# The w_out product as seven block products in a one-core encoder step

## The chip, the cores and the metric

The kernel runs on one core of one Trainium2 chip. The metric is the device time of one execution in microseconds (us). One core has five engines that work at once: TensorE (PE, matrix products into PSUM banks), VectorE (DVE), ScalarE (ACT), GpSimd (POOL) and SyncE (SP), which here only issues transfers (DMAs). Each engine, and each queue of DMAs, takes its own instructions in a fixed order.

## The reference

One layer of a streaming encoder over 1024 prompt tokens and 64 sample tokens: norm, one input projection, two attention branches, and then the part that matters here:

```python
def merge_and_ffn(x, oa, ob, ga, gb, w_o_a, w_o_b, w_out, norm_ffn, w_up, w_down):
    B, T, _ = x.shape
    m = ga * (oa.reshape(B, T, W_A) @ w_o_a) + gb * (ob.reshape(B, T, W_B) @ w_o_b)
    x = x + m @ w_out
    h = jnp.square(jax.nn.relu(rmsnorm(x, norm_ffn) @ w_up))
    return x + h @ w_down
```

`m` and `x` have 1024 + 64 rows of 1024, `w_out` is 1024 x 1024, and everything is float32.

## The kernel before

A float32 product is made of three passes: each operand is split into a rounded part `hi` and the rest `lo` (`split`, L145: ACT copies to `hi`, then POOL or DVE subtracts to get `lo`), and `three` (L152) issues hi·hi, hi·lo and lo·hi for each block of 128 in the inner dimension k. The 64 sample rows are held as hi and lo side by side in one block of 128 columns ("few"), so they need two passes.

The stages around the change, in order of time:

- **Merge** (L960 to L989). For each block m of 128 model columns and each of three chunks of tokens, two products into the PSUM tile `acc` (six banks), a DVE multiplication by each gate (L978), a POOL sum of the two branches (L981), and a split of the sum into `mT` (L988 on ACT, L989 on DVE).
- **Out product** (L1063 to L1093). `together` takes 512 columns of w_out at a time, and for each of eight blocks k runs all row tiles of a group: rows 0 to 3 and the sample rows, or rows 4 to 7 (a row tile is 128 tokens). `in_turn` takes the last two strips of 256 columns for rows 4 to 7, one row tile after the other. Weights come through the pool `ring`: `raw` has 3 buffers, `hi` and `lo` 5 each; POOL makes `lo`. `take` adds a finished PSUM tile to the residual tile `x1[i]` on DVE (L1057).
- **Norm and transposes** (`ffn_columns`, L1023). A row tile whose 1024 columns are complete is stored, squared and summed on ACT (L172), scaled on DVE (L174), transposed by PE in two groups of four (L1034, PSUM tile `pt`, two banks), and ACT copies each group twice: to `turned` (two buffers), which a DMA on ACT's queue stores, and, for rows 0 to 3 and the first 32 sample rows, to the operands B11 and B21 of the next product (names with `xB`), whose `lo` DVE makes (L1042).
- **Up product** (L1109 on). It is already a product by seven blocks. Its first products, in the PSUM tiles `pf`, `pa` and `pe`, need B11 complete: rows 0 to 3 and the sample rows. Rows 4 to 7 are only needed much later.

The order of instructions on each engine is set when the kernel is built, by a scheduler that may move an instruction ahead of others that it takes to be waiting; the pools decide which buffer a tile gets, and thereby what it waits for.

## Time and profile before

| what | us |
| --- | --- |
| median of 3 runs (1688.88 to 1691.14) | 1690.06 |
| the profiled execution | 1689.98 |
| its span, first to last instruction | 1687.8 |
| PE busy in the span | 1671.8 |
| first matmul of the out product, from the span's start | 910.54 |
| first matmul of the up product | 1011.64 |

All times of the trace count from the span's start. What an execution takes beyond the span is 1689.98 - 1687.8 = 2.2 us. A row of the timeline gives the start, the duration, the engine, the line and the operation, out<-in; a matmul's duration overlaps the next one's, so what a matmul costs is read from one start to the next. A row of the stages gives the busy time of each engine between two times, then the granted TensorE clock (1.00 is full speed), the share of the DMA engines and the GB/s. "DMA to landing" is the time from the issue of a transfer to its arrival.

### The profile page before, as it was taken

To read this page: it belongs to the slowest core of one execution; us is meant where nothing else is said; L and a number is where in the kernel's file an instruction comes from. 1 tells how busy PE (TensorE), PEld (TensorE's weight loads), DVE (VectorE), ACT (ScalarE), POOL (GpSimd) and SP (SyncE) were. 2 spreads that over 40 slices of the span, in tenths; PEclk is the share of its full clock that TensorE was granted. 3 is DMA by queue.
4 is the path that set the end of the run, shared out by engine and by line. 5 is a ranking of instruction groups with operands and counts; after the bars stand their busy time and mean duration, and the time that the engine had idled before them with its cause. 6 is when DMAs were issued, how large, how long until landed. Compare 5 with 4: busy or idle time off the path is not lost.

```text
span 1687.8 us, 29807 instructions
## 1 busy us (share of the span) xinstructions
PE 1671.8 (99%) x10181; PEld 1525.1 (90%) x10181; DVE 1165.4 (69%) x2732; ACT 936.1 (55%) x1874; POOL 388.6 (23%) x524
## 2 busy tenths in 40 slices
PE   9899999999999999999999999999999999999999
PEld 8887888888989999999999899999999988888887
DVE  6854899878868788873553346756687649656794
ACT  6866578795167777774443446544454346443431
POOL 4344223504533434332344430000000000000000
PEclk9999999999999999999999999999999999999999
DMA  7234365673498876645545459555565598765652
GB/s 248 62 123 136 99 182 161 181 252 100 114 217 205 201 178 158 161 113 177 166 136 168 171 168 303 170 178 178 188 223 188 191 294 300 238 202 172 204 187 87
DMA packets 278119, 303.06 MB, mean 180 GB/s; under 512 B 40208, under 2 KB 196368, under 8 KB 277968
## 3 DMA queue, kind: packets, MB, share of 16 engines
q1 hardware_dynamic: 248704, 265.44, 53.6%
q10 hardware_dynamic: 29264, 35.73, 6.0%
q8 instruction: 80, 1.31, 0.3%
q14 instruction: 71, 0.58, 0.1%
HBM read 207.98 MB, written 93.08 MB: 178 GB/s over the span
## 4 chain that ended last, share of the span: by engine, by line
PE 79%; DMA 3%; DVE 3%; issue 1%; POOL 1%; ACT 1%; SPq 0%; DVEq 0%; ACTq 0%; POOLq 0%
PE acc L156 7%; PE acc L158 7%; PE acc L157 7%; PE x L158 6%; PE x L157 6%; PE x L156 6%; PE pt L817 3%; PE wide L158 2%; PE wide L157 2%; PE wide L156 2%; PE pg L156 2%; PE pg L158 2%; PE pg L157 2%; PE pe L156 2%; PE pe L158 2%; PE po L833 2%
## 5 line engine op out<-in xcount | busy, mean ns | idle before, releaser
L124 ACT ACTIVATE hi<-hw 128x1024 fp32r<-128x1024 f32 (+1 forms) x108 | 100.2, 933 | 158.3 <-PE x L158 51.0
L157 PE MATMUL x<-lo,hi 128*128 128x512 f32 (+1 forms) x440 | 169.5, 385 | 0.0
L158 PE MATMUL x<-hi,lo 128*128 128x512 f32 (+1 forms) x440 | 169.1, 385 | 0.0
L156 PE MATMUL x<-hi 128*128 128x512 f32 (+1 forms) x440 | 165.1, 385 | 0.0
L148 DVE TENSOR_TENSOR lo<-hw,hi 128x1024 fp32r<-128x1024 f32 (+1 forms) x108 | 114.0, 1061 | 48.6 <-ACT hi L124 46.5
L150 POOL TENSOR_TENSOR lo<-raw,hi 128x512 fp32r<-128x512 f32 x74 | 96.9, 1315 | 127.0 <-ACT hi L124 112.4
L124 ACT ACTIVATE hi<-raw 128x512 fp32r<-128x512 f32 x104 | 65.1, 627 | 91.1 <-PE acc L157 21.6
L622 ACT ACTIVATE nth<-work,cand 128x768 bf16<-128x768 f32 (+2 forms) x93 | 96.6, 1038 | 15.9 <-DVE cand L640 9.6
L829 DVE TENSOR_TENSOR pl<-pt,ph 128x512 fp32r<-128x512 f32 (+2 forms) x152 | 91.6, 616 | 14.5 <-ACT ph L124 14.0
L157 PEld LDWEIGHTS x<-lo,hi 128*128 128x128 f32 x440 | 82.7, 188 | 16.6
L156 PEld LDWEIGHTS x<-hi 128*128 128x128 f32 x440 | 82.6, 188 | 16.7 <-ACT hi L124 0.2
L158 PEld LDWEIGHTS x<-hi,lo 128*128 128x128 f32 x440 | 82.6, 188 | 16.5
L156 PE MATMUL acc<-xnT,hi 128*128 128x384 f32 (+1 forms) x288 | 96.2, 334 | 0.2 <-DVE gate L688 0.2
L124 ACT ACTIVATE ph<-pt 128x512 fp32r<-128x512 f32 (+3 forms) x168 | 80.9, 514 | 26.1 <-PE pt L817 16.4
L158 PE MATMUL acc<-xnT,lo 128*128 128x384 f32 (+1 forms) x288 | 94.3, 327 | 0.0
L157 PE MATMUL wide<-wlo,xnT 128*128 128x512 f32 x240 | 94.2, 394 | 0.0
L157 PE MATMUL acc<-xnT,hi 128*128 128x384 f32 (+1 forms) x288 | 94.2, 327 | 0.0
L158 PE MATMUL wide<-whi,xnT 128*128 128x512 f32 x240 | 93.8, 391 | 0.0
L156 PE MATMUL wide<-whi,xnT 128*128 128x512 f32 x240 | 92.2, 394 | 0.9 <-DVE work_s L383 0.9
L804 POOL TENSOR_SCALAR mw<-mw,sm 128x640 f32<-128x640 f32 (+1 forms) x64 | 56.6, 885 | 122.7 <-DVE sm L803 118.3
L833 PE MATMUL po<-pl,vhl 128*128 128x256 f32 (+1 forms) x304 | 79.0, 291 | 0.7 <-DVE pl L829 0.7
L832 PE MATMUL po<-ph,vhl 128*128 128x256 f32 (+1 forms) x304 | 78.6, 275 | 0.3 <-ACT ph L124 0.2
(700 smaller groups left out, 5612.0 us busy)
## 6 DMA issues: line engine op xcount, KB each, us to landing
hw<-h SPq DMA_DIRECT2D x108, 256.0 KB, 3.1
hw<-in_w_down_dram SPq DMA_DIRECT2D x108, 256.0 KB, 3.5
wraw<-in_w_in_dram SPq DMA_DIRECT2D x56, 256.0 KB, 2.8
h<-h ACTq DMA_DIRECT2D x32, 272.0 KB, 2.1
raw<-in_w_out_dram SPq DMA_DIRECT2D x32, 256.0 KB, 2.7
raw<-in_w_up_dram SPq DMA_DIRECT2D x32, 256.0 KB, 3.1
out_dram<-t SPq DMA_DIRECT2D x24, 256.0 KB, 2.5
raw<-in_w_in_dram SPq DMA_DIRECT2D x24, 256.0 KB, 3.6
```

Source lines behind the costliest of these rows:

```text
L124: return nc.scalar.activation(out, in_, AF.Copy)
L148: last["lo"] = nc.vector.tensor_sub(lo, raw, hi)
L150: nc.gpsimd.tensor_sub(lo, raw, hi)
L156: nc.tensor.matmul(out, sh, mh, start=(opens and i == 0), stop=False, skip_group_check=resumes)
L157: nc.tensor.matmul(out, sh, ml, start=False, stop=False, skip_group_check=resumes)
L158: last = nc.tensor.matmul(out, sl, mh, start=False, stop=(closes and i == n - 1), skip_group_check=resumes)
L622: nc.scalar.activation(sign[:, :w.shape[1]], w, AF.Sign, bias=against, scale=-1.0, accum_out=col(cnt, j))
L804: nc.gpsimd.tensor_scalar(m[:rows, :n], m[:rows, :n], sm[:rows, 6:7], 1.0, op0=ALU.mult, op1=ALU.mult)
L817: nc.tensor.transpose(ps[:krows, oo:oo + qrows], m[:qrows, kc:kc + krows], ident[:qrows, :qrows])
L829: nc.vector.tensor_sub(pl[:kr, a:b], ps[:kr, a:b], ph[:kr, a:b])
L832: nc.tensor.matmul(dst, vhl[:krows, vt, :], ph[:krows, oo:oo + width], start=(idx == 0), stop=False)
L833: nc.tensor.matmul(dst, vhl[:krows, vt, :], pl[:krows, oo:oo + width], start=False, stop=(idx == n - 1))
```

## The change

The 1024 prompt rows of `m`, and w_out, are cut into two by two blocks of 512. Instead of eight block products, seven are made: P1 and P2 from the blocks themselves, the other five from sums of left blocks and sums of right blocks. Each is four row tiles by 512 columns by four blocks k. They run in the order P1, P2, P6, P5, P3, P7, P4; P1, P6, P5, P3 follow each other in the same four PSUM banks without being cleared, so that a bank holds P1, then P1 + P6, and so on, and DVE adds it to the rows that need it at each stage (`into`). P2 goes through the two `pt` banks. P7 and P4 are chained in the same way. The sample rows keep eight small matmuls a block product, in P1, P2, P3 and P7.

The sums of left blocks are made in the merge stage by DVE (`left_sums`, after each pair of blocks m), from `m_of`, which keeps `m` unsplit; they are split one block product ahead of their use (`left_side`). The sums of right blocks are made from the freshly loaded weights (`right_side`); `t1_of` and `t2_of` keep two of them from one product to the next. The residual rows are loaded by `load_rows`, rows 0 to 3 and the sample rows with P1, rows 4 to 7 with P2. All of rows 4 to 7 now get their last addition only from P4, and all four are normed behind it. Some pools change sides.

On DVE, at the end of the merge stage (`gta` and `gtb` are the gates, `m_...` the kept blocks of `m`, `x_0` the first residual row tile), before:

```order
L978 TENSOR_TENSOR gta<-acc,gta 128x320
L989 TENSOR_TENSOR mT_11321<-gtb,mT_11321 128x256
L989 TENSOR_TENSOR mT_11322<-gtb,mT_11322 128x64
L1057 TENSOR_TENSOR x_0_12353<-acc,x_0_12353 128x512
L1057 TENSOR_TENSOR x_1_12354<-acc,x_1_12354 128x512
```

and after (`tc` is a tile of `t1_of`, `raw` a block of w_out):

```order
L1002 TENSOR_TENSOR gta<-acc,gta 128x320
L961 TENSOR_TENSOR s_3_11337<-m_11329,m_11333 128x512
L965 TENSOR_TENSOR m_11329<-m_11329,m_11333 128x64
L955 TENSOR_TENSOR few_m<-m_11333,few_m 128x64
L962 TENSOR_TENSOR m_11329<-m_11329 128x512
L955 TENSOR_TENSOR few_m<-m_11329,few_m 128x64
L963 TENSOR_TENSOR m_11329<-s_3_11337,m_11329 128x512
L148 TENSOR_TENSOR lo<-m_11326,hi 128x512
L1105 TENSOR_TENSOR tc<-tc,raw 128x512
```

The last reader of P1's first block of weights (L1105) now stands behind the left sums of the last pair.

On SP's queue, from the w_out blocks of the first product on (`x_0` to `x_8` are the residual row tiles, `x_8` the sample rows), before:

```order
L1050 DMA raw<-in_w_out_dram 128x512 x4
L1009 DMA x_0_12353<-in_x_prompt_dram 128x1024
L1009 DMA x_1_12354<-in_x_prompt_dram 128x1024
L1009 DMA x_2_12355<-in_x_prompt_dram 128x1024
L1009 DMA x_3_12356<-in_x_prompt_dram 128x1024
L1011 DMA x_8_12357<-in_x_sample_dram 64x1024
L1009 DMA x_4_12349<-in_x_prompt_dram 128x1024
L1009 DMA x_5_12350<-in_x_prompt_dram 128x1024
L1009 DMA x_6_12351<-in_x_prompt_dram 128x1024
L1009 DMA x_7_12352<-in_x_prompt_dram 128x1024
L1050 DMA raw<-in_w_out_dram 128x512 x14
```

and after:

```order
L1040 DMA tc<-in_w_out_dram 128x512 x4
L1034 DMA x_0_12344<-in_x_prompt_dram 128x1024
L1034 DMA x_1_12345<-in_x_prompt_dram 128x1024
L1034 DMA x_2_12346<-in_x_prompt_dram 128x1024
L1040 DMA raw<-in_w_out_dram 128x512
L1034 DMA x_3_12347<-in_x_prompt_dram 128x1024
L1036 DMA x_8_12348<-in_x_sample_dram 64x1024
L1034 DMA x_4_12340<-in_x_prompt_dram 128x1024
L1034 DMA x_5_12341<-in_x_prompt_dram 128x1024
L1034 DMA x_6_12342<-in_x_prompt_dram 128x1024
L1034 DMA x_7_12343<-in_x_prompt_dram 128x1024
L1040 DMA raw<-in_w_out_dram 128x512 x16
```

Before, all eight blocks k of the first pass stand ahead of the residual rows. After, P1's fourth block stands between `x_2` and `x_3`, and all of P2's blocks behind `x_7`.

On PE, at the end of the out product (`pt` are transposes, `pf` the first up product), before:

```order
L158 MATMUL acc<-hi,mT_11321 128x256
L1034 MATMUL pt<-ident,xg 128x128 x8
L156 MATMUL pf<-xB_of_x,hi 128x272
L157 MATMUL pf<-xB_of_x,hi 128x272
L158 MATMUL pf<-xB_of_x,lo 128x272
```

and after:

```order
L158 MATMUL acc<-hi,lo 128x512
L1067 MATMUL pt<-ident,xg 128x128 x16
L1067 MATMUL pt<-ident,xg 128x64 x8
L156 MATMUL pf<-xB_of_x,hi 128x272
L157 MATMUL pf<-xB_of_x,hi 128x272
L158 MATMUL pf<-xB_of_x,lo 128x272
```

Before, the eight transposes there are of row tile 4, which the up product does not need yet. After, row tiles 2 and 3 and the sample rows are transposed between the last block product and the up product, which needs them. On ACT, in the same place after (`junk` is the square of a row tile, `sd` its root, `hi` a weight of the up product):

```order
L172 ACTIVATE junk,ss<-x_5_12341 128x1024
L124 ACTIVATE hi<-raw 128x512 x2
L132 ACTIVATE sd<-ss,eps 128x1
L124 ACTIVATE turned<-pt 128x512
L124 ACTIVATE xB_of_x<-pt 128x4x128
L172 ACTIVATE junk,ss<-x_6_12342 128x1024
L124 ACTIVATE turned<-pt 128x512
L124 ACTIVATE xB_of_x<-pt 128x4x128
L132 ACTIVATE sd<-ss,eps 128x1
L172 ACTIVATE junk,ss<-x_7_12343 128x1024
L1077 DMA xT_74<-turned 128x8x128
L124 ACTIVATE turned<-pt 128x512
```

The copies of row tile 2 (the `turned` and `xB` rows here) stand among the squares of row tiles 5, 6 and 7; row tile 3 and the sample rows follow.

The core of the diff:

```diff
+    pairs_of_m = tuple(m for k in range(4) for m in (k, k + 4))
...
+    def left_sums(k):
+        a, b = m_of[k], m_of[k + 4]
+        a1, a2, b1, b2 = a[:, :512], a[:, 512:1024], b[:, :512], b[:, 512:1024]
+        nc.vector.tensor_add(s1_of[k], a2, b2)
+        nc.vector.tensor_sub(a2, a1, a2)
+        nc.vector.tensor_sub(a1, s1_of[k], a1)
+        nc.vector.tensor_sub(b1, b1, a1)
+        nc.vector.tensor_add(a[:, 1024:], a[:, 1024:], b[:, 1024:])
+        few_block(2, k, a[:, 1024:])
...
+            nc.gpsimd.tensor_add(m_of[m][:, c0:c0 + n], prods[1][:, :n], prods[0][:, :n])
+            if ci == 1:
+                hi, lo = (row_blocks["A11" if m < 4 else "A12"][:, m % 4, z] for z in range(2))
+                copied = copy(hi, m_of[m][:, :512])
+                nc.vector.tensor_sub(lo, m_of[m][:, :512], hi)
+            elif ci == 2:
+                copied = few_block(m // 4, m % 4, m_of[m][:, 1024:])
+                if m >= 4:
+                    left_sums(m - 4)
...
+    def right_side(nm, k):
+        hi = ring.tile([P, 512], F32R, tag="hi", name="hi", bufs=RING)
+        lo = ring.tile([P, 512], F32R, tag="lo", name="lo", bufs=RING)
+        if nm == "P1":
+            t = out_block(k, 0, 0)
+            out_block(k, 0, 1, t1_of[k])
...
+        split(t, hi, lo)
+        if nm == "P1":
+            nc.vector.tensor_sub(t1_of[k], t1_of[k], t)
+        return hi, lo
...
+    ops = sides("P1")
+    load_rows(first_rows)
+    sums, few_sum = [acc() for _ in range(4)], acc()
+    by_halves(sums, ops, True, (few_sum, 0, True))
+    for t in range(4):
+        into(t, 0, sums[t])
+    ops = sides("P2")
+    load_rows(second_rows)
+    for t in range(4):
+        ps = ptile()
+        tile_product(ps, t, ops, range(4), True)
+        into(t, 0, ps)
...
+    sums = [acc() for _ in range(4)]
+    by_halves(sums, sides("P7"), True, (few_sum, 3, False))
+    for t in range(2):
+        ffn_columns(t)
+    ops = sides("P4")
+    for t in range(2, 4):
+        ffn_columns(t)
+    into(NT, 1, few_sum)
+    ffn_columns(NT)
+    for t in range(4):
+        into(4 + t, 1, sums[t])
+    by_halves(sums, ops, False)
+    for t in range(4):
+        into(4 + t, 0, sums[t])
...
-    together(first_rows, 0)
-    together(first_rows, 512)
-    together(second_rows, 0)
-    in_turn(second_rows, 512)
-    in_turn(second_rows, 768)
...
     with tc.issue_after(begin(0, "pf").ins):
+        ffn_columns(4)
         ffn_columns(5)
```

## The prediction

> **What bounds the kernel now.** I read the page first, then the stages around the out product, then the timeline of single engines there.

> ```profile
> span 1687.8 us, 29807 instructions
> PE 1671.8 (99%) x10181; PEld 1525.1 (90%) x10181; DVE 1165.4 (69%) x2732; ACT 936.1 (55%) x1874; POOL 388.6 (23%) x524
> ```

> PE is the bound by share, and the stages say that this holds here too. The rows are the merge, the out product and the start of the up product; after the stretch stand its length, then PE's busy time, PE's weight loads, DVE, ACT, POOL, the granted clock, the share of the DMA engines and GB/s.

> ```profile
> 820.00:912.90 92.90, 92.90 (x564) 92.48 (x563) 49.99 (x90) 39.75 (x99) 45.59 (x42) 1.00 0.42 128
> 912.90:1011.00 98.10, 98.10 (x545) 85.41 (x544) 34.12 (x77) 41.45 (x81) 38.15 (x30) 1.00 0.59 194
> 1011.00:1030.00 19.00, 18.92 (x156) 18.54 (x154) 10.19 (x21) 11.78 (x23) 0.67 (x1) 1.00 0.85 245
> ```

> PE has no gap in the out product and 0.08 us after it, at full clock. So every matmul that goes is won in full, and every wait that comes is lost in full. The matmuls' prices come from starts in PE's timeline (start, duration, what):

> ```profile
> 910.54 0.39 PE L156 MATMUL acc<-hi,mT 128*128 128x512 f32 x1
> ...
> 929.61 0.39 PE L156 MATMUL acc<-hi,mT 128*128 128x512 f32 x1
> ...
> 931.88 0.39 PE L157 MATMUL acc<-lo,mT 128*128 128x512 f32 x1
> ...
> 985.80 0.28 PE L156 MATMUL acc<-hi,mT 128*128 128x256 f32 x1
> ...
> 988.80 0.28 PE L157 MATMUL acc<-lo,mT 128*128 128x256 f32 x1
> ...
> 1010.85 1.04 PE L1034 MATMUL pt<-ident,xg 128*128 128x128 f32 x8
> 1011.64 0.37 PE L156 MATMUL pf<-xB_of_x,hi 128*128 128x272 f32 x1
> ```

> Ten 512-wide matmuls take 931.88 - 929.61 = 2.27, so 0.227 each; 25 of 256 columns take 3.00, so 0.120 each; eight transposes take 0.79.

> **The change: PE's work.** Before, 288 matmuls of 512 columns (96 for each `together`), 192 of 256 (`in_turn`) and 32 for the sample rows: 320 x 0.227 + 192 x 0.120 = 72.6 + 23.0 = 95.6 us. After, seven products of 48, and the same 32: 368 x 0.227 = 83.5. **Gain 12.1 us.** The transposes stay 72.

> **Work added on the other engines.** Each product from P6 on splits four left blocks and makes most of its right ones: per 10.9 us of PE some 8 ACT copies, 12 DVE operations and 4 POOL subtractions.

> ```profile
> L124 ACT ACTIVATE hi<-raw x38: 615/632/655, 908.8 to 1026.8; 128x512 fp32r<-128x512 f32 x38
> L150 POOL TENSOR_TENSOR lo<-raw,hi x31: 1283/1294/2132, 909.5 to 1010.4; 128x512 fp32r<-128x512 f32 x31
> 985.43 0.67 DVE L1057 TENSOR_TENSOR x<-acc,x 128x512 f32<-128x512 f32 x1
> 986.03 0.67 DVE L1042 TENSOR_TENSOR xB_of_x<-pt,xB_of_x 128x512 fp32r<-128x512 f32 x1
> L174 DVE SCALAR_TENSOR_TENSOR xg<-x,rs,g_ffn x9: 1271/1283/1553, 962.6 to 1018.7; 128x1024 f32<-128x1024 f32 x8, 64x1024 f32<-64x1024 f32 x1
> ```

> That is 8 x 0.63 = 5.0 us of ACT, 12 x 0.60 (starts 0.60 apart) = 7.2 of DVE, 4 x 1.29 = 5.2 of POOL: hidden under the matmuls. Five buffers for four blocks and the halves of `by_halves` let the next product's first blocks be split while the second half runs (24 matmuls, 5.4 us, against 0.63 + 1.29). I take 0; if that cover goes, each seam costs up to 1.9. The left sums add four operations of 0.60 for each of four pairs to DVE, which is busy 50 of 92.9 us in the merge: 0 there. The chained banks make PE wait for `into` of a tile, 0.67, but 18 other matmuls (4.1 us) stand between: 0. The sides of pools and the deferred sample rows cost 0.

> **The seam P1 to P2.** This is where the order hurts. Rows of the merge's end and of the loads before:

> ```profile
> 911.25 0.48 DVE L978 TENSOR_TENSOR gta<-acc,gta 128x320 f32<-128x320 f32 x1
> 912.55 0.87 POOL L981 TENSOR_TENSOR gtb<-gta,gtb 128x320 f32<-128x320 f32 x1
> 914.04 1.28 ACT L991 ACT_TABLE_LOAD   x1
> 913.04 1.81 SPq L1009 DMA_DIRECT2D x<-in_x_prompt_dram  x4
> 915.88 6.12 SPq L1009 DMA_DIRECT2D x<-in_x_prompt_dram  x4
> 922.10 2.78 SPq L1050 DMA_DIRECT2D raw<-in_w_out_dram  x3
> 932.91 1.95 ACT L124 ACTIVATE hi<-raw 128x512 fp32r<-128x512 f32 x3 [12.16 <-DMA raw<-in_w_out_dram]
> DMA to landing us min/median/max: 2.5/2.6/10.9
> 920.00:922.00 2.00, 2.00 (x11) 1.65 (x10) 0.00 (x0) 0.63 (x1) 0.83 (x1) 1.00 1.01 401
> 922.00:926.00 4.00, 4.00 (x20) 3.30 (x19) 0.00 (x0) 0.00 (x0) 0.46 (x1) 1.00 1.05 223
> 926.00:930.00 4.00, 4.00 (x19) 3.34 (x18) 0.00 (x0) 0.00 (x0) 0.00 (x0) 1.00 1.02 398
> ```

> A w_out block issued behind the residual rows at 922.10 is there at 932.9, 10.8 us later; one alone takes 2.6. Before, this hid behind eight blocks of PE work (25 us). Now only P1 (56 matmuls, 12.7 us) stands ahead of P2.

> P1's fourth block needs the first one's `raw` buffer, which L1105 on DVE frees last. That waits behind the last left sums: last gate product until 911.73, POOL's sum 0.87, until 912.7; two DVE operations and two small ones, until 914.3; the second of two `few_m` splits waits for ACT, which loads a table first (1.28 and two short operations from 913.0), until 915.0; then L963, a `lo` and L1105, until 916.9. SP is held there with all that is queued behind: x_3, x_8, x_4 to x_7, P2's blocks. From 917.0, 0.26 + 0.52 + 0.26 + 2.10 + 0.26 = 3.4 MB (a row tile is 128 x 1024 x 4 bytes) pass until P2's first block is in: 8.5 us at 400 GB/s, up to 10.3 with a dip like that of 922 to 926, and 2.6 - 0.65 = 1.9 of latency: 927.4 to 929.2, up to 1 later with the gains of the norm (0.5 MB on ACT's queue). I take 928.9; then 0.1 + 0.63 for `hi`: PE starts P2 at 929.6.

> P1 ends at 910.54 + 12.7 = 923.2 without waits. Its fourth block lands at 919.6 to 920.3, its `hi` is ready at 920.3 to 921, when PE has reached it (42 matmuls, 920.1), and `lo` 1.3 later, against 5 matmuls: 0.9 in all (0.5 to 1.5). So P1 ends at 924.1 and **P2 waits 5.5** (4.0 to 6.8); its `lo` comes 1.4 after `hi`, against three matmuls: 0.7 more (0.5 to 0.9). **Sum 7.1 us** (5.0 to 9.2).

> **The seam P4 to the up product.** 24 transposes now stand behind P4, and the up product needs their copies. ACT's prices:

> ```profile
> 964.76 1.04 ACT L172 ACTIVATE junk<-x 128x1024 bf16<-128x1024 f32 x1
> 966.13 1.04 ACT L172 ACTIVATE junk<-x 64x1024 bf16<-64x1024 f32 x1
> 969.02 0.60 ACT L124 ACTIVATE turned<-pt 128x512 f32<-128x512 f32 x1 [0.45 <-PE pt L1034]
> 969.51 0.59 ACT L124 ACTIVATE xB_of_x<-pt 128x512 fp32r<-128x512 f32 x1
> DMA to landing us min/median/max: 3.2/3.9/6.8
> ```

> A square with its root takes 1.37, a copy 0.49. Call P4's last matmul 0. ACT's queue from -0.7 on (the second residual addition of row tile 5): three squares with roots (4.1), a further root (0.2), two weight copies (1.1), eight copies of row tiles 2 and 3 (3.9), issues (0.3): done at 8.9. With two `pt` banks PE cannot run ahead. Then the sample rows' copy into `turned` needs the buffer of row tile 2, whose store is issued only behind the square of row tile 7, at 6.6, and lands 3.2 to 6.8 later; I take 4.3, a little over the median, since four row stores run beside it: 10.9. Two short copies, DVE's `lo` and the wake-ups: the up product starts at 11.9. Of that, 24 transposes are work (16 at 0.10 and 8 small ones, some 2.5): **9.4 us of wait**. Without the buffer it would be 9.9 - 2.5 - 0.5 = 6.9; with the slowest landing 10.9 or so. Rows 4 to 7 that follow are hidden as rows 5 to 7 were.

> **The clock after a gap.** In the first stages PE has gaps:

> ```profile
> 48.00:52.00 4.00, 2.26 (x16) 1.95 (x15) 3.72 (x25) 3.78 (x12) 2.01 (x11) 1.00 0.46 163
> 52.00:56.00 4.00, 4.00 (x30) 3.99 (x29) 3.93 (x16) 2.10 (x6) 0.09 (x1) 1.00 0.09 15
> 56.00:60.00 4.00, 2.42 (x16) 1.86 (x14) 3.80 (x12) 4.00 (x14) 3.23 (x11) 1.00 0.12 27
> 60.00:64.00 4.00, 3.41 (x20) 3.18 (x18) 3.68 (x12) 4.00 (x11) 0.24 (x2) 0.69 0.00 0
> 64.00:68.00 4.00, 4.00 (x24) 3.81 (x24) 2.93 (x12) 2.62 (x8) 0.00 (x0) 0.88 0.00 0
> ```

> After 3.3 idle us of 12, the clock was 0.69 and 0.88 for two stretches of 4: 1.24 + 0.48 = 1.7 us lost. Both seams have gaps of that kind; the first may absorb its share in waits for `lo`. I take 1.7 once (0 to 3.4). [...]

> **The sum.** -12.1 + 7.1 + 9.4 + 1.7 = +6.1 us, on the profiled execution's own 1689.98 (0.08 below the median): **1696.1**. With all bounds low -12.1 + 5.0 + 6.9 = -0.2 (1689.8), with all high -12.1 + 9.2 + 10.9 + 3.4 = +11.4 (1701.4).

> **The rivals.**
> - *Neither seam shows* (the full gain): the blocks and B11 come in time. For it: PE is the bound by share, and DMA is busy only 0.59 here. Against it: the 10.8 us behind the residual rows. 1689.98 - 12.1 = 1677.9.
> - *P2's blocks come in time*, if DVE gets to L1105 early or the first rows leave little ahead: -12.1 + 9.4 + 1.7 = -1.0, 1689.0.
> - *The end is covered*, if the squares of rows 5 to 7 fall in ACT's idle time: -12.1 + 7.1 + 1.7 = -3.3, 1686.7.
> - *DVE becomes the bound in P7 and P4*: 104 matmuls and 16 transposes are 25.2 us of PE; DVE has 30 operations of 0.60 there, four of 1.28 for `xg` and some 25 small ones of about 0.2: 28.1. Then 2.9 more: 1699.0. Against it: much of that is off PE's path.

> **How the numbers follow.** 0.2%, 3.4 us, is about what a measurement of this kernel can tell from no change. Forecast 0.58, neither 0.09, only the end 0.13, only the first seam 0.12, DVE besides 0.08. Slower by over 3.4: the forecast's part above +3.4 (0.49) and DVE (0.08): 0.57. Within: the rest of the forecast (0.09), most of *only the end* (0.11), half of *only the first seam* (0.06): 0.26. Faster: 0.09, 0.06 and 0.02: 0.17. The range 1686 to 1701 leaves out *neither* (0.09), the lower part of *only the first seam* (0.04) and the top (0.05).

> **What would show it.** In the profile after: a gap of PE of about 6 us some 13 us behind the out product's start, ended by ACT's `hi` and a w_out DMA; a gap between P4 and `pf` broken by transposes, with ACT full; granted clock below 1.00 behind either. I am wrong if P2 starts right behind P1, if B11 is complete before P4 ends, or if the stage from 910.54 to `pf` takes under 101.1 us - 3.4.

## The result, and the profile after

The changed kernel takes 1698.16 us (median of 4 runs, 1697.35 to 1700.79) against 1689.47 us before: ratio 1.0053, 95% interval 1.0036 to 1.0071, so 6.1 to 12.0 us slower. The forecast was 1696.1, in a range of 1686 to 1701. The profiled execution took 1697.35. Its page:

```profile
span 1695.6 us, 29545 instructions
PE 1664.2 (98%) x10037; PEld 1513.8 (89%) x10037; DVE 1200.0 (71%) x2777; ACT 938.0 (55%) x1870; POOL 387.4 (23%) x520
```

PE is busy 7.6 us less than before and the span is 7.8 us longer: PE waits. All its waits from 905 to 1030 us, as the list of waits gives them (line, what it waited for, us in total, times, longest):

```profile
PE pt L156 <- ACT hi L124: 6.8, 1, 6.8
PE pt L1067 <- DVE ms L131: 3.3, 1, 3.3
PE pt L1067 <- DVE r L133: 3.3, 2, 2.1
PE acc L156 <- ACT hi L124: 1.5, 1, 1.5
```

PE's timeline shows where they lie (start, duration, what, the idle time just before it and what ended that):

```profile
909.03 0.39 PE L156 MATMUL acc<-hi,m_A 128*128 128x512 f32 x1
...
920.41 1.20 PE L156 MATMUL acc<-hi,m_A 128*128 128x512 f32 x4 [1.53 <-ACT hi L124]
...
923.80 0.40 PE L1132 MATMUL acc<-lo,few_m 128*128 128x512 f32 x1
931.04 1.22 PE L156 MATMUL pt<-hi,m_A 128*128 128x512 f32 x2 [6.85 <-ACT hi L124]
...
936.32 0.39 PE L158 MATMUL pt<-hi,m_A 128*128 128x512 f32 x1
...
1006.15 0.39 PE L158 MATMUL acc<-hi,lo 128*128 128x512 f32 x1
1006.41 0.63 PE L1067 MATMUL pt<-ident,xg 128*128 128x128 f32 x4
1008.27 0.63 PE L1067 MATMUL pt<-ident,xg 128*128 128x128 f32 x4 [1.23 <-DVE r L133]
1012.24 1.96 PE L1067 MATMUL pt<-ident,xg 128*128 128x128 f32 x8 [3.34 <-DVE ms L131]
1016.26 1.32 PE L1067 MATMUL pt<-ident,xg 64*128 64x64 f32 x8 [2.07 <-DVE r L133]
1017.51 0.59 PE L156 MATMUL pf<-xB_of_x,hi 128*128 128x272 f32 x1
```

P1 begins at 909.03, waits 1.53 for its fourth block, P2 waits 6.85 for its first one, and behind P4 three waits stand between the transposes until the up product begins at 1017.51. Before, the same stretch (first matmul of the out product to the first of the up product) was 910.54 to 1011.64: 101.10; now it is 108.48, 7.4 longer. Ahead of it the two profiles differ by 1.5 us the other way, behind it by another 1.9: 7.4 - 1.5 + 1.9 = 7.8, the difference of the spans. The 1.5 is not of the change: over the twelve kernels below, with the same program ahead up to the end of the merge, the out product began anywhere from 908.87 to 913.53. So they are compared from its first matmul on.

The 1.9 behind it, and more of the stretch, is clock. The stages of the changed kernel (length, PE, weight loads, DVE, ACT, POOL, granted clock, DMA share, GB/s):

```profile
924.00:931.00 7.00, 0.20 (x1) 0.00 (x0) 1.09 (x2) 0.63 (x1) 0.00 (x0) 0.88 0.94 365
931.00:936.00 5.00, 4.96 (x12) 3.66 (x13) 0.00 (x0) 1.88 (x3) 3.92 (x4) 0.50 0.33 110
...
1017.50:1021.50 4.00, 4.00 (x18) 3.99 (x18) 1.68 (x3) 0.87 (x4) 0.00 (x0) 0.50 0.73 143
1021.50:1030.00 8.50, 8.50 (x73) 8.50 (x72) 3.77 (x4) 4.28 (x8) 0.00 (x0) 1.00 0.48 137
```

After both gaps PE works at half clock (0.50). P2's first twelve matmuls take 936.32 - 931.04 = 5.28 where twelve take 2.8 at full clock: 2.5 lost, the small waits for `lo` among them included. The up product loses another 1.8 (16 matmuls in 3.80, at 0.125 each 2.0).

### The profile page after: what moved, and what is told of

Read it like the earlier page. It is cut to its first block, busy times and chain, and to the rows that moved or that the text cites. A ratio compares the mean times of both kernels' runs of the same rounds, so it can differ in the third digit from the quotient of the medians.

```text
span 1695.6 us, 29545 instructions
## 1 busy us (share of the span) xinstructions
PE 1664.2 (98%) x10037; PEld 1513.8 (89%) x10037; DVE 1200.0 (71%) x2777; ACT 938.0 (55%) x1870; POOL 387.4 (23%) x520
## 3 DMA queue, kind: packets, MB, share of 16 engines
q8 instruction: 79, 1.29, 0.3%
## 4 chain that ended last, share of the span: by engine, by line
PE 70%; DMA 4%; DVE 3%; issue 1%; ACT 1%; POOL 1%; SPq 0%; DVEq 0%; POOLq 0%; ACTq 0%
PE x L156 6%; PE x L157 6%; PE x L158 6%; PE acc L156 5%; PE acc L157 5%; PE acc L158 5%; PE pt L817 3%; PE pg L156 2%; PE pe L156 2%; PE pe L158 2%; PE pg L158 2%; PE pe L157 2%; PE pg L157 2%; PE po L833 2%; PE s L164 2%; PE s L165 2%
## 5 line engine op out<-in xcount | busy, mean ns | idle before, releaser
L124 ACT ACTIVATE hi<-hw 128x1024 fp32r<-128x1024 f32 (+1 forms) x108 | 100.4, 933 | 161.3 <-PE x L158 50.1
L157 PE MATMUL x<-lo,hi 128*128 128x512 f32 (+1 forms) x440 | 169.5, 385 | 0.0
L156 PE MATMUL x<-hi 128*128 128x512 f32 (+1 forms) x440 | 164.7, 385 | 0.0
L150 POOL TENSOR_TENSOR lo<-raw,hi 128x512 fp32r<-128x512 f32 x62 | 84.4, 1366 | 111.3 <-ACT hi L124 95.5
L124 ACT ACTIVATE hi<-raw 128x512 fp32r<-128x512 f32 x92 | 57.1, 625 | 87.9 <-issue 17.6
L829 DVE TENSOR_TENSOR pl<-pt,ph 128x512 fp32r<-128x512 f32 (+2 forms) x152 | 91.5, 615 | 14.5 <-ACT ph L124 14.0
L156 PEld LDWEIGHTS x<-hi 128*128 128x128 f32 x440 | 82.7, 188 | 16.6
L157 PEld LDWEIGHTS x<-lo,hi 128*128 128x128 f32 x440 | 82.7, 188 | 16.5
L156 PE MATMUL acc<-xnT,hi 128*128 128x384 f32 (+1 forms) x288 | 96.3, 334 | 0.2 <-DVE gate L688 0.2
L124 ACT ACTIVATE ph<-pt 128x512 fp32r<-128x512 f32 (+3 forms) x168 | 80.9, 514 | 26.2 <-PE pt L817 16.5
L157 PE MATMUL acc<-xnT,hi 128*128 128x384 f32 (+1 forms) x288 | 94.3, 327 | 0.0
L157 PE MATMUL wide<-wlo,xnT 128*128 128x512 f32 x240 | 94.2, 394 | 0.0
L156 PE MATMUL wide<-whi,xnT 128*128 128x512 f32 x240 | 92.2, 394 | 0.6 <-DVE work_s L383 0.6
```

The source lines that it names most:

```text
L124: return nc.scalar.activation(out, in_, AF.Copy)
L150: nc.gpsimd.tensor_sub(lo, raw, hi)
L156: nc.tensor.matmul(out, sh, mh, start=(opens and i == 0), stop=False, skip_group_check=resumes)
L157: nc.tensor.matmul(out, sh, ml, start=False, stop=False, skip_group_check=resumes)
L829: nc.vector.tensor_sub(pl[:kr, a:b], ps[:kr, a:b], ph[:kr, a:b])
```

## The experiments

Theory when they began: two seams and the clock, as predicted. Rival for the first seam: something else than the residual rows holds the queue. Rival for the end: another engine than ACT. Each row of the table is one profiled execution; "stretch" runs from P1's first matmul (before: the first of the out product) to the first of the up product, "to the end" from P1's first matmul to the end of the span; the ratio is that of the measured times to the kernel before, with its 95% interval.

| kernel | P2 starts after | P4's end to up product | stretch | to the end | ratio |
| --- | --- | --- | --- | --- | --- |
| before | | 0.8 | 101.10 | 777.3 | 1 |
| changed | 22.01 | 11.13 | 108.48 | 786.6 | 1.0053 [1.0036, 1.0071] |
| rows late | 15.48 | 11.14 | 101.59 | 780.3 | 1.0021 [1.0010, 1.0031] |
| gains late | 21.25 | 11.16 | 108.20 | 786.7 | 1.0049 [1.0033, 1.0065] |
| filled | 23.04 | 11.15 | 109.24 | 787.2 | 1.0054 [1.0035, 1.0073] |
| filled behind P1 | 23.20 | 11.39 | 109.96 | 788.2 | 1.0054 [1.0034, 1.0074] |
| woven | 21.71 | 0 | 103.59 | 779.8 | 1.0012 [1.0003, 1.0022] |
| squares late | 21.46 | 10.01 | 107.31 | 785.2 | 1.0048 [1.0032, 1.0064] |
| own buffer | 22.29 | 11.13 | 108.87 | 787.0 | 1.0044 [1.0028, 1.0059] |
| three edits | 15.14 | 0 | 97.60 | 773.8 | 0.9973 [0.9958, 0.9988] |
| left sums late | 15.72 | 0 | 97.39 | 773.5 | 0.9967 [0.9956, 0.9979] |
| L1105 first | 12.91 | 0 | 96.44 | 772.6 | 0.9975 [0.9965, 0.9984] |
| shifted | 14.61 | 0 | 99.19 | 775.4 | 0.9979 [0.9970, 0.9987] |
| lows on POOL | 12.92 | 0 | 99.34 | 778.1 | 1.0004 [0.9992, 1.0016] |

**Residual rows behind P2's blocks** (rows late).

```diff
     ops = sides("P2")
-    load_rows(second_rows)
+    with tc.issue_after(last["block"].ins):
+        load_rows(second_rows)
```

> The changed kernel with the residual rows 4 to 7 queued behind the four w_out blocks of P2 instead of ahead of them; nothing else is changed. If P2 waits because 2 MB of rows pass ahead of its weights, its first block goes behind x_3 and the sample rows alone (0.75 MB, issued 10 us after P1's first matmul), is in some 13.5 to 14.5 us after that matmul, and PE waits 0 to 1 us there instead of 6.85; the clock drop behind the gap (2.4 us) goes too: about 1689 (8 to 9 less than the changed kernel). Rival: the queue is held by something else (the third buffer of raw, or the gains), so that P2's blocks come as late as before: 1696 to 1698. A second rival: the rows now come too late for their additions behind P6: the wait moves there, 1692 to 1697.

Measured: 1694.43 us, P2's wait is

```profile
929.01 0.72 PE L156 MATMUL pt<-hi,m_A 128*128 128x512 f32 x2 [1.23 <-ACT hi L124]
```

instead of 6.85, and its matmuls run at full clock (1.00). The stretch is 6.9 shorter. So it is the 2 MB of residual rows ahead of P2's blocks that cost most of the first seam, with the clock behind it. The whole fell by 5.4 us by the two ratios, not by the 8 to 9 expected: the wait for P1's fourth block stayed (0.60), so did 1.23 for P2's first, and new small ones came (0.40 and 0.75 for `lo`).

**Gains out of the way** (gains late): how SP was held, read from the changed kernel. SP's queue:

```profile
914.76 0.33 SPq L1040 DMA_DIRECT2D raw<-in_w_out_dram  x1
919.01 0.33 SPq L1034 DMA_DIRECT2D x<-in_x_prompt_dram  x1
919.39 0.50 SPq L1036 DMA_DIRECT2D x<-in_x_sample_dram  x1
919.93 2.01 SPq L1034 DMA_DIRECT2D x<-in_x_prompt_dram  x4
922.05 13.12 SPq L1040 DMA_DIRECT2D raw<-in_w_out_dram  x6
```

P1's fourth block goes out at 914.76, x_3 only at 919.01, with SP idle between. ACT's queue, what SP waited for there, and the stage in which the DMA engines ran dry:

```profile
910.73 0.38 ACTq L1054 DMA_DIRECT2D g_ffn<-in_norm_ffn_dram  x1
```

```profile
SPq L1034 <- DMA g_ffn<-in_norm_ffn_dram: 3.9, 1, 3.9
```

```profile
918.00:920.00 2.00, 0.88 (x4) 0.38 (x2) 1.17 (x3) 0.27 (x1) 0.00 (x0) 1.00 0.06 19
```

The gains took 8.3 to land, and 910.73 + 8.3 = 919.03: x_3 goes out when the gains are there. Why a transfer on SP's queue waits for one on ACT's is not in the trace.

```diff
-    nc.scalar.dma_start(g_ffn, bcast(norm_ffn, D))
...
+    with tc.issue_after(last["row"].ins):
+        ops = sides("P2")
+    with tc.issue_after(last["block"].ins):
+        nc.sync.dma_start(g_ffn, bcast(norm_ffn, D))
```

> The changed kernel with the gains of the norm (0.5 MB, before on ACT's queue, issued 1.7 us after P1's first matmul and landing 8.3 us later) loaded on SP's queue behind P2's blocks; SP's order of the other loads stays: P1's fourth block, x_3, sample rows, x_4 to x_7, P2's blocks. In the changed kernel SP issued nothing between P1's fourth block (5.7 us after P1's first matmul) and x_3 (10.0), although no buffer of x_3 was in use: x_3 went out when the gains had landed. If the landing of the gains holds the queue, x_3 now goes at 5.8 to 6.5, P2 starts 17 to 18 us after P1's first matmul instead of 22.0, and the time is 1692 to 1693.5. Rival: L1105 on DVE or the bytes alone set it; then only 0.5 MB less are ahead, 1.3 us: 1696.

Measured: 1698.55 us. SP's queue now, and two stages of that kernel:

```profile
915.44 0.33 SPq L1040 DMA_DIRECT2D raw<-in_w_out_dram  x1
915.82 0.42 SPq L1034 DMA_DIRECT2D x<-in_x_prompt_dram  x1
```

```profile
920.00:922.00 2.00, 2.00 (x9) 1.34 (x8) 0.17 (x1) 0.00 (x0) 1.00 (x1) 1.00 1.01 217
...
926.00:928.00 2.00, 0.00 (x0) 0.00 (x0) 0.00 (x0) 0.00 (x0) 0.00 (x0) 0.54 1.03 386
```

The hold is real and gone (x_3 follows its predecessor at once), and it gave little: P2 starts 21.25 after P1's first matmul instead of 22.01. The rival came nearer: x_3 goes out 3.0 sooner, but from there to the split of P2's first block 13.6 pass instead of 11.4, with only 217 GB/s in one of these stages, against 386 in the other. The run takes the hold and the 0.5 MB of gains away together, so it does not tell the two apart.

**Matmuls in the gap** (filled): 28 spare matmuls of 512 columns between P1 and P2.

```diff
+    spare = ptile()
+    for _ in range(28):
+        nc.tensor.matmul(spare, row_blocks["A11"][:, 0, 0, :128], row_blocks["A11"][:, 0, 0], start=True, stop=True)
```

> The changed kernel with 28 more matmuls of 512 columns (28 x 0.23 = 6.4 us, operands that are ready, into a bank that P2 clears later) put on PE between P1 and P2, inside the gap of 6.85. They add no work that the result needs. If the clock is lowered because PE was idle, P2's first 12 matmuls go at 0.23 instead of 0.43 each: 2.4 us less, about 1695. Rival: these matmuls are slow for another reason (weights that are split late, full DMA queues): no change, 1697 to 1698.

Measured: 1699.52 us. The scheduler put them ahead of P1's last quarter; P2 still waited 3.62 and its next matmuls still took 0.43 each. So a gap of 3.6 drops the clock too (to 0.50), for 3.4 us where the gap of 6.85 dropped it for 6.8; the theory wasn't tested. The next run holds them behind P1's last matmul.

```diff
+    with tc.issue_after(last["few"].ins):
+        for _ in range(28):
+            filled = nc.tensor.matmul(spare, ...)
...
+        with tc.issue_after(filled.ins):
+            tile_product(ps, t, ops, range(4), True)
```

> As the run with 28 extra matmuls, but now held on PE behind P1's last matmul and ahead of P2's first, where the gap of 6.85 lies (in the earlier run they went ahead of P1's last quarter, and a gap of 3.62 was left behind that). If the clock is lowered by PE's idle time, P2's first matmuls now go at 0.23, and from P1's first matmul to P4's last it takes 95.0 instead of 97.35; the whole 1695 to 1696. Rival: they stay at 0.43 (97.3 in the stage; the whole 1698).

Measured: 1699.63 us. PE's timeline there:

```profile
924.72 6.53 PE L1160 MATMUL pt<-m_A 128*128 128x512 f32 x28
932.77 0.50 PE L156 MATMUL pt<-hi,m_A 128*128 128x512 f32 x1 [1.53 <-ACT hi L124]
934.13 0.50 PE L157 MATMUL pt<-lo,m_A 128*128 128x512 f32 x1 [0.63 <-POOL lo L150]
```

P2 came 1.2 later than in the changed kernel, two waits of 1.53 and 0.63 were left, and the clock fell behind these to 0.50, for 3.4 us instead of 6.8. The expectation failed, and this run alone doesn't tell idle time from other causes; the last section sets all gaps side by side.

**Transposes woven into P7 and P4** (woven). PE's order is held: what follows a row's transposes is issued after them.

```diff
+                if (ks[0], t) in rows_at:
+                    ffn_columns(rows_at[ks[0], t])
+                    held.enter_context(tc.issue_after(last["turn"].ins))
...
-    by_halves(sums, sides("P7"), True, (few_sum, 3, False))
...
+    by_halves(sums, sides("P7"), True, (few_sum, 3, False), {(0, 2): 0, (2, 1): 1})
...
-    by_halves(sums, ops, False)
+    by_halves(sums, ops, False, None, {(0, 0): 2, (0, 3): 3, (2, 2): NT})
```

> The changed kernel with the transposes of row tile 0 in the middle of P7, of 1 near its end, of 2 and 3 in P4's first half and of the sample rows in P4's second half: PE's order is held there, the work is the same. If the end waits because the transposes of rows 2, 3 and the sample rows stand behind P4, and the engines that prepare them have time before, the 11.1 us from P4's last matmul to the up product shrink to 1 to 3, and the clock drop behind (1.8) goes: 1686 to 1688. Rival: the chain of squares, scaling and copies on ACT and DVE is itself the bound, and PE now waits inside P7 and P4 for what it waited for behind them: 1694 to 1698.

Measured: 1691.75 us. The up product follows P4 without a gap, at full clock (0.125 from start to start): what follows the stretch takes 676.2, as before the change. PE waits five times for DVE's subtractions inside P7 and P4, 2.6 us in all. So the place of the transposes costs the end, some 7 us with the clock; a part of what it gave went back at the first seam, where a wait of 1.88 in P1 halved the clock in this profile.

**Squares of rows 4 to 7 later** (squares late) and **a buffer of its own for the sample rows** (own buffer): the two parts into which my prediction had split the end.

```diff
-    with tc.issue_after(begin(0, "pf").ins):
+    last["ours"] = last["turned"]
+    with tc.issue_after(begin(0, "pf").ins), tc.issue_after(last["ours"].ins):
```

> The changed kernel with the squares and roots of row tiles 4 to 7 held on ACT's queue behind the copies of the sample rows, which the up product needs. My prediction put three squares with roots (4.1 us) into the wait behind P4. If ACT's queue is what PE waits for there, the 11.1 us from P4's last matmul to the up product shrink to 7 to 8.5, and the whole to 1694.5 to 1696. Rival: the buffers of the scaled rows and of the transposes set it (DVE scales the sample rows only when row 2's transposes have freed its buffer), and ACT merely has its work in between: 10 to 11 us stay, 1697 to 1698.5.

```diff
-        raw = npool.tile([P, KB, P], F32, tag="turned", name="turned", bufs=2)
+        if i < NT:
+            raw = npool.tile([P, KB, P], F32, tag="turned", name="turned", bufs=2)
+        else:
+            raw = chain_tile().rearrange("p (k r) -> p k r", k=KB)
```

> The changed kernel with a buffer of its own for the turned sample rows (one of the tiles that hold sums of right blocks, free by then), so that they don't wait for the store of row tile 2. My prediction gave that wait 2.0 us of the end (11.9 with it, 9.9 without). If so, the 11.1 us from P4's last matmul to the up product become 9 to 9.5. Rival: the sample rows' transposes themselves come late (they ended at 1017.5 minus 0.6 us in the changed kernel, the copy began at 1017.37), so that only 0.4 to 0.8 go: 10.3 to 10.7. Either way the whole stays within 2 us of the changed kernel: 1696 to 1698.

Measured: 1697.6 and 1698.71 us. Without the squares in ACT's queue the end shrinks from 11.13 to 10.01; with the extra buffer it stays at 11.13, although the trace of the changed kernel had put a wait of 1.77 on that buffer. For the squares the rival came true; the buffer gave less than even its rival had (10.3 to 10.7). Neither was the bound. PE's row and ACT's in the run without the squares, with what ended their idle time:

```profile
1012.17 1.94 PE L1067 MATMUL pt<-ident,xg 128*128 128x128 f32 x8 [3.56 <-DVE xB_of_x L1075]
```

```profile
1013.29 0.60 ACT L124 ACTIVATE turned<-pt 128x512 f32<-128x512 f32 x1 [3.56 <-PE pt L1067]
```

ACT stands idle there for as long as PE, and PE waits for DVE. DVE's queue at that place in the changed kernel:

```profile
1008.12 0.66 DVE L1145 TENSOR_TENSOR x<-acc,x 128x512 f32<-128x512 f32 x1
...
1008.89 0.67 DVE L148 TENSOR_TENSOR lo<-raw,hi 128x512 fp32r<-128x512 f32 x1
1009.50 1.27 DVE L174 SCALAR_TENSOR_TENSOR xg<-x,rs,g_ffn 64x1024 f32<-64x1024 f32 x1
...
1010.76 0.67 DVE L148 TENSOR_TENSOR lo<-raw,hi 128x512 fp32r<-128x512 f32 x1
...
1011.43 0.66 DVE L1075 TENSOR_TENSOR xB_of_x<-pt,xB_of_x 128x512 fp32r<-128x512 f32 x1
...
1014.24 1.28 DVE L174 SCALAR_TENSOR_TENSOR xg<-x,rs,g_ffn 128x1024 f32<-128x1024 f32 x1 [0.34 <-PE pt L1067]
1015.44 0.68 DVE L1075 TENSOR_TENSOR xB_of_x<-pt,xB_of_x 128x512 fp32r<-128x512 f32 x1
```

A bank of transposes is free only when DVE's subtraction L1075 has read it. The one at 1011.43, behind an addition, two splits and the scaling of the sample rows, frees the bank for the transposes at 1012.24; the one at 1015.44, behind the scaling of row 4, those at 1016.26. (The list of waits puts these down to small DVE operations, `ms` and `r`, that ended at about the same time.) No run takes DVE's work out of this place alone, so this reading rests on the timelines.

**Three edits together.** Rows 4 to 7 and the gains behind P2's blocks, and the woven order as above.

```diff
-    nc.scalar.dma_start(g_ffn, bcast(norm_ffn, D))
...
+    with tc.issue_after(last["block"].ins):
+        load_rows(second_rows)
+    with tc.issue_after(last["row"].ins):
+        nc.sync.dma_start(g_ffn, bcast(norm_ffn, D))
```

> Three edits together: P2's blocks ahead of the residual rows 4 to 7, the gains behind them, and the transposes woven into P7 and P4. If the two seams are separate causes, their parts add: apart, they took the stretch from P1's first matmul to the up product from 108.48 to 101.59 and to 103.59, and the second took 1.9 off what follows; together 96.7, what follows 676.2, the whole 1683 to 1686, some 5 us under the kernel before. Rival: the waits are one chain (what the first seam gives back is waited for at the end, since DVE and ACT have to do the same work in less time): stretch 100 to 102, the whole 1688 to 1691.

Measured: 1686.02 us, ratio 0.9973 [0.9958, 0.9988], stretch 97.60. The parts add to within 1 us: apart they took 6.9 and 4.9 off 108.48, which would give 96.7. That they come so near is in part luck: in this kernel x_3 and the sample rows also stand ahead of P1's fourth block, which cost a wait of 3.75 in P1 and 3.4 us of half clock, and P2 then ran without a wait for its first block. This version beats both kernels. The next two take DVE's work ahead of L1105 away: first the last left sums, then also the splits of P6's left blocks, which had taken their place.

```diff
-                if m >= 4:
+                if 4 <= m < 7:
                     left_sums(m - 4)
...
+    with tc.issue_after(last["t1"].ins):
+        left_sums(3)
```

> As the three edits together, and DVE's left sums of the last pair stand behind L1105, whose end frees the buffers for P1's fourth block and P2's blocks. If L1105 behind the left sums holds these loads, P1's fourth block goes out some 2.5 us earlier and P2's blocks 4 or more, the waits left in the first seam (0.6 + 1.2 + 0.4 us with the rows moved) go: 1681 to 1684, stretch 94 to 95. Rival: x_0 to x_2 that pass ahead, and not the buffers, set it: no difference to the three edits.

```diff
+        with tc.issue_after(last["t1"].ins) if nm == "P6" else ExitStack():
+            split(src, hi, lo, lo_on_vector=True)
```

> As the three edits with the left sums behind L1105, and DVE's splits of P6's left blocks (which wait for ACT, that loads a table first) behind L1105 too, since in the run before these had taken the place of the left sums: L1105's first came at 5.2 us after P1's first matmul, P1's fourth block at 6.0. If DVE's order is what holds P1's fourth block and P2's blocks, L1105 now comes at 2.5 to 3.5, the fourth block goes out ahead of x_2, the waits of the first seam (2.5 us and a clock drop of 1.7) go, and the stretch from P1's first matmul to the up product is 93 to 94 (97.4 before), the whole 1681 to 1683. Rival: the loads are late for their bytes: no change, 1684 to 1686.

Measured: 1685.19 and 1687.12 us, not to be told apart, and both above what was expected; with the left sums late the stretch is that of the three edits (97.39). Where L1105 comes first, P1's fourth block goes out 2.9 after P1's first matmul (5.7 in the changed kernel), P1 runs without a wait (P2 at 12.91: 56 matmuls at 0.231), P2 with one of 0.22, and the clock stays up (1.00). L1105 did hold these loads. But the stretch shrinks by 1 only. All PE's waits there from 905 to 1010:

```profile
PE pt L1066 <- DVE xB_of_x L1074: 3.3, 3, 1.4
PE pt L1066 <- DVE xg L174: 1.8, 1, 1.8
PE acc L157 <- POOL lo L150: 0.5, 1, 0.5
PE pt L157 <- POOL lo L150: 0.2, 1, 0.2
```

DVE's work of P7 and P4 is next: what PE no longer waits for at the seam it waits for there (5.1 us, against 2.7 with the left sums late). Two runs tried that. In the first (shifted) rows 1, 2 and 3 are transposed one row tile of matmuls later.

```diff
-{(0, 2): 0, (2, 1): 1}
+{(0, 2): 0, (2, 2): 1}
...
-{(0, 0): 2, (0, 3): 3, (2, 2): NT}
+{(0, 1): 2, (2, 0): 3, (2, 2): NT}
```

> As the run with L1105 first, and the transposes of row tiles 1, 2 and 3 each one row tile of matmuls later (1.4 us), since they waited 0.3 to 1.1 us each for DVE to free their bank. If DVE is only late by that, these waits (2.6 us in all) mostly go: 1 to 2 us less than that run. Rival: DVE has the same queue at each place, the waits move along: no difference over 0.5 us.

Measured: 1687.98 us; the waits move along, as the rival said (5.4 us in P7 and P4 instead of 5.1). The stretch is 2.8 longer in that profile, 1.7 of it ahead of P2, where nothing was edited. In the second (lows on POOL) the subtractions L1075 go to POOL.

```diff
-                nc.vector.tensor_sub(dst[:, :, 1], v[:, :, r0:r1], dst[:, :, 0])
+                nc.gpsimd.tensor_sub(dst[:, :, 1], raw[:, 4 * j:4 * j + 4, r0:r1], dst[:, :, 0])
```

> As the run with L1105 first; the ten subtractions that make the low parts of the up product's operands (rows 0 to 3 and the sample rows) are moved from DVE, where they read the transposes' PSUM bank, to POOL, where they read ACT's copy `turned`; PE's order is the same, row by row. So a bank of transposes is free after ACT's two copies. If DVE's queue is what PE waits for at the transposes (three waits of 1.39, 1.39 and 0.50 us ended by these subtractions, and 1.80 for the scaled row 0), the first three go: the stretch from P1's first matmul to the up product is 92.5 to 94 instead of 96.4, the whole some 3 us less than that run. Rival: ACT's copies are as late as DVE's subtractions, or POOL (1.3 us each) makes the low parts too late for the up product: 95.5 to 97.

Measured: 1692.65 us. The three waits for the subtractions are gone, and a new one of 4.14 has come, for DVE's addition that frees P4's first bank; the stretch is 2.9 longer, outside both ranges. The up product, once begun, waits another 0.86 and 1.07 for copies and low parts, as the second half of the rival said. DVE and POOL in that kernel:

```profile
985.32 2.39 DVE L174 SCALAR_TENSOR_TENSOR xg<-x,rs,g_ffn 128x1024 f32<-128x1024 f32 x1
...
989.69 1.28 DVE L174 SCALAR_TENSOR_TENSOR xg<-x,rs,g_ffn 128x1024 f32<-128x1024 f32 x1
```

```profile
984.08 2.55 POOL L1074 TENSOR_TENSOR xB_of_x<-turned,xB_of_x 128x512 fp32r<-128x512 f32 x2
986.59 2.25 POOL L150 TENSOR_TENSOR lo<-raw,hi 128x512 fp32r<-128x512 f32 x1
```

The same scaling takes 2.39 where it begins while a POOL operation runs (985.32) and 1.28 where POOL stands idle as it begins (989.69). Work taken from DVE came back as longer operations of DVE.

## Why the prediction was right, and where it was wrong

**The gain** (12.1). Right. In the changed kernel a matmul of 512 columns costs 0.231 in P1 and P2 and 0.226 from P6 on (the last 26 starts ahead of 1001.4: 5.66 for 25). 112 and 256 of them make 83.8 against the 83.5 forecast: 11.8 of gain.

**The first seam** (7.1; 5.0 to 9.2). Mechanism right, size low. 1.53 + 6.85, and 0.4 for the late `lo` of P1's fourth block (14 matmuls in 3.62, at 0.231 3.24): 8.8. L1105 freed the first buffer 5.7 after P1's first matmul, 6.4 were forecast. P1's fourth block went out then, but its split began 5.0 later, where 2.6 to 3.3 were forecast. The step that failed for P2 is the hold of SP's queue: the prediction let the gains cost up to 1 as bytes, and x_3 went out at 10.0 instead of 6.5, while the DMA engines ran dry (share 0.06 from 918 to 920). From x_3 to the split of P2's first block 11.4 then passed, no more than forecast. But the 400 GB/s would have failed without the hold: in the run with the gains late these bytes took 13.6, and P2 came only 0.8 sooner.

**The end** (9.4; 6.9 to 10.9). Size right by luck, cause wrong. From P4's last matmul 11.1 passed where 11.9 were forecast; less 2.5 of transposes that is 8.6: 6.6 of listed waits, and 2.0 by which the transposes took longer, most of them at half clock. ACT's queue was done at 9.2, close to the 8.9 forecast, but the step that made it PE's path failed: the squares are worth 1.1, the buffer of row tile 2, put at 2.0, nothing. The last step failed too. The up product does not wait for the copies of the sample rows, as the prediction and the text ahead of it have it: it began at 1017.51, straight behind their transposes, and its first matmuls read columns of row tiles 0 to 2. ACT's first copy of sample rows for it came later:

```profile
1017.65 0.27 ACT L124 ACTIVATE xB_of_x<-pt 128x128 fp32r<-128x128 f32 x1
```

So the place of the transposes in PE's order set the end, and with it, as the timelines read, DVE's queue, through the subtractions that free the banks of transposes. The prediction had counted those banks ("With two `pt` banks PE cannot run ahead") and let ACT free them.

**The clock** (1.7, once). Right that it falls, wrong in size: both gaps cost, 2.5 and 1.8, 4.3 together, more than the upper bound of 3.4. The row from the first stages was read as a sum over gaps; here the drop is one of 6.8 and 10.2 us at half clock behind the two gaps (granted clock 0.50), over P2's matmuls in the one, over transposes and the up product's matmuls in the other.

**The sum.** -11.8 + 8.8 + 8.6 + 4.3 = +9.9, against 786.6 - 777.3 = +9.3 from the first matmul to the end and +8.7 between the medians. The forecast of +6.1 was low by the first seam (1.7) and the clock (2.6).

**The rivals.** *Neither seam* is out. *Only the end* and *only the first seam* are out, and each exists as a kernel: rows late (+0.2%) and woven (+0.1%) come out 3.8 and 1.1 us above the kernel before, where these cases gave 1.0 and 3.3 below it, since clock and smaller waits stay. *DVE as the bound* wasn't so here (no gap of PE in P7 and P4), and is so once the seams are closed: 5.1 us of waits in the kernel with L1105 first. The full gain of 12 us was reached by none; the best lost some 8 of it (stretch 96.4; 101.1 less 11.8, and less 0.8 for the transposes of row 4 that moved behind, would be 88.5). PE's waits make 5.8 of that; where the other 2 went is open.

## What to carry to other kernels

The 11.8 us of matmuls that the change took away here came with 8.7 us more of time. Fewer matmuls shorten the time only where everything that fed the longer product is also ready for the shorter one: look at what stands in each queue ahead of the first operand of the next product, in bytes, at what else that queue waits for, and at what stands behind the last. A bank of transposes came free here, as the timelines read, with its last reader (DVE's subtraction L1075 from 1015.44, 0.68 long; the next transposes at 1016.26): follow that reader's queue, not the one that looks busiest. The two gaps of PE here cost more than their length, since the clock was at 0.50 behind each (2.5 and 1.8 us lost).

## What the runs showed of the hardware

```profile
1011.00:1011.50 0.50, 0.00 (x0) 0.00 (x0) 0.50 (x3) 0.50 (x3) 0.00 (x0) 0.79 1.00 401
...
1021.00:1021.50 0.50, 0.50 (x4) 0.50 (x3) 0.00 (x0) 0.00 (x0) 0.00 (x0) 0.50 0.05 7
1021.50:1022.00 0.50, 0.50 (x6) 0.50 (x5) 0.00 (x0) 0.00 (x0) 0.00 (x0) 0.97 0.00 0
```

It lasts from 1011.29 to 1021.53, 10.2 us; the first one, read likewise, 6.8; two in the woven kernel 3.4 and 6.8. The spacing of PE's matmuls shows 18 drops in these kernels from 905 to 1025; the ten of which the stages show both ends last 3.4 (six), 6.8 (two) or 10.2 (two). Waits of 1.53, 1.63 (1.23 and 0.40), 1.68, 1.81 and 1.93 (0.86 and 1.07, lows on POOL) left the clock at 1.00; waits of 1.83 (1.44 and 0.39), 1.88, 2.16 (1.53 and 0.63) and every single one from 3.3 up halved it. So there is no sharp bound between 1.8 and 2.0. The woven kernel, where 1.88 did:

```profile
922.50:923.50 1.00, 0.92 (x4) 0.79 (x5) 0.10 (x1) 0.03 (x1) 0.84 (x1) 1.00 0.79 242
...
924.00:926.50 2.50, 2.49 (x7) 2.01 (x7) 1.07 (x2) 0.00 (x0) 0.00 (x0) 0.50 1.03 316
```

PE is back at work at 922.58 and the clock falls 1.4 us later. Since the fill runs left waits of their own, idle time as the cause rests on this comparison.

**Side by side, operations of DVE and POOL took longer.** In the kernel with the lows on POOL, the three scalings that began while a POOL operation ran took 2.14 to 2.39, the two that began while POOL stood idle 1.28; an operation on 128 x 1 (L137) took 1.08 instead of 0.14. POOL's `lo` beside a scaling took 2.25 there, 1.28 in the quickest case before.

**Ahead of the sample rows' landing the DMA rate was about half.** In the six kernels of which the stages there are read microsecond by microsecond (before, changed, rows late, gains late, three edits, L1105 first) it fell to 170 to 260 GB/s, at a DMA share of 0.84 or more, for one to three us within the five ahead of the landing of the tile of 64 rows, wherever that stood in the queue (217 GB/s in the stage shown, 386 in the other). No run separates that tile from what else was under way, so what lowers the rate is not shown.
